# Down projections of a two-layer diffusion backbone as seven products instead of eight

## The chip, the cores and the metric

One core of one Trainium2 chip runs the whole program. The metric is the device time of one execution in microseconds (us). A profile of one execution gives the start and the length of every instruction on the engines: TensorE (PE; its weight loads are PEld), VectorE (DVE), ScalarE (ACT), GpSimd (POOL) and SyncE (SP).

## The reference, cut to what matters

The network has two layers over 512 latent tokens and 256 context tokens, 768 in all, with a width D of 1024. Each layer is a feed-forward half, a token mixer and a second feed-forward half. All three are modulated and normalised alike. The feed-forward part has 2816 features, in 22 tiles of 128:

```python
def _ffn_sublayer(h, shift, scale, gate, g_pre, g_post, w_gate, w_up, w_down):
    u = _modulate(_rmsnorm(h, g_pre), shift, scale)
    y = (jax.nn.silu(u @ w_gate) * (u @ w_up)) @ w_down
    return h + FFN_RES * gate * _rmsnorm(y, g_post)
```

The last layer's mixer and second feed-forward part need the 512 latent tokens alone. So of the four feed-forward parts three work on 768 tokens and the last on 512.

## The kernel before

Every float32 product runs as three passes: each operand is split into a leading part `hi`, made by a copy on ScalarE, and the rest `lo`, made by a subtraction on VectorE. TensorE then sums hi x hi, hi x lo and lo x hi in PSUM. Function `halves` (L191) does one split; `weights` (L177) loads a block of 128 rows and splits it 512 columns at a time.

A feed-forward part (`ffn`, L527) has two stages.

*Gate and up.* The first two feature tiles are ordinary products. The other twenty go through `strassen` (L588), two tiles at a time, by seven products in place of eight: the blocks are feature tile by half of D on one side and half of D by chunk of tokens on the other. A chunk is 384 tokens (256 in the last part). One `job` (L606) is one pair of tiles for gate or for up: two loads of weights, three splits, four sums of weights on VectorE, four more splits, seven products of 12 matmuls with 384 columns, and copies and sums of the results. 20 jobs make up a stage. Each feature tile's h goes to DRAM (`hd`).

*Down.* `type2` (L665) takes one chunk of tokens after the other. For each of the 22 feature tiles it loads 128 rows of `w_down` and the chunk's h from `hd`, splits both, and adds three passes into three accumulators of [128 tokens, 1024], 18 matmuls of 512 columns. The last four feature tiles (`STAG`) are held back and run token tile by token tile, so that the three token tiles of a chunk finish 24 matmuls apart. The last feed-forward part takes its four token tiles jointly.

*Boundary.* When a token tile is finished, `boundary` (L494) squares its two halves on ScalarE, multiplies them by the gate's row on VectorE, takes the root on GpSimd, and returns the rest: load x, add, store x, normalise (`normed`, L407: a square on ScalarE, a scaling on GpSimd), and `make_u` (L375): eight transposes on TensorE (`turned`, L416), shift and scale on ScalarE and VectorE, and the split into the next stage's u. The first chunk's rests are run between feature tiles of the second chunk (`later`); the second chunk's at once, beside the next stage's first products. Where the next stage is a feed-forward part, `Sums` (L422) also makes the differences of u that its seven products take; `prepare` adds hi and lo of the first chunk up again on GpSimd.

The order of instructions on each engine is chosen at compile time by a scheduler, from priorities and from when operands are ready. `late` (L81) makes an instruction keep its place behind those issued before it on its queue. Loads and the stores of h go through SyncE's queue; loads and stores of x and the gate's rows go through GpSimd's.

## Time and profile before

| | |
|---|---|
| device time, median of 3 runs | 2635.53 us (2626.84 to 2635.57) |
| span of the profiled execution | 2636.3 us |
| TensorE busy | 2546.2 us (97%) |
| VectorE busy | 1757.5 us (67%) |
| ScalarE busy | 1351.8 us (51%) |
| mean DMA rate | 153 GB/s |

The span runs from the first to the last instruction of the program, on the same clock as the device time. Busy time is the union of an engine's instructions; TensorE's overlap, and their ends are modelled.

### The profile page before, as it was taken

Reading aid. Unit: us, or ns where it says so; the run is one execution under the profiler, and the core shown is the slowest. Engines: PE = TensorE matmul, PEld = TensorE weight load, DVE = VectorE, ACT = ScalarE, POOL = GpSimd, SP = SyncE. Lnnn points to the kernel's source line nnn. Section 1 sums busy time; section 2 is a strip of 40 time slices with the busy share of each in tenths; the row PEclk is TensorE's granted clock in tenths of the full one; section 3 lists DMA queues with packets and bytes.
Section 4 is the critical chain, followed back from the end, with each engine's and each line's share of the span. In section 5 each row is a group of like instructions: output and inputs, shape, how many; then the busy total and the mean of one; then the engine's idle time right before and its main releaser. Section 6 shows DMA issues by size and latency. Waiting matters only on the chain.

```text
span 2636.3 us, 38740 instructions
## 1 busy us (share of the span) xinstructions
PE 2546.2 (97%) x13980; PEld 2237.5 (85%) x13980; DVE 1757.5 (67%) x3199; ACT 1351.8 (51%) x2783; POOL 325.3 (12%) x356
## 2 busy tenths in 40 slices
PE   7999999999999999999999999999999899899998
PEld 5899998889855789999888899998887667799986
DVE  5766664658777686767555767665557657899843
ACT  4444444547566654444454544444545556666632
POOL 4000000213022240000011300000122221400000
PEclk8999999999999999999999999999999999999999
DMA  7445436541387443232555332235554552544542
GB/s 275 144 160 168 152 127 206 192 160 53 119 293 266 157 141 96 96 105 100 187 184 189 124 97 95 98 107 177 198 181 152 200 176 82 177 135 128 161 167 88
DMA packets 147761, 403.00 MB, mean 153 GB/s; under 512 B 16504, under 2 KB 33576, under 8 KB 147568
## 3 DMA queue, kind: packets, MB, share of 16 engines
q1 hardware_dynamic: 136688, 362.00, 41.6%
q0 software_dynamic: 10880, 38.53, 4.2%
q8 instruction: 109, 1.79, 0.3%
q14 instruction: 84, 0.69, 0.1%
HBM read 351.91 MB, written 48.55 MB: 152 GB/s over the span
## 4 chain that ended last, share of the span: by engine, by line
PE 80%; DVE 7%; issue 5%; ACT 3%; POOL 3%; DMA 2%; POOLq 0%; DVEq 0%; ACTq 0%; SPq 0%
PE px L601 17%; PE py L601 12%; PE pz L601 12%; PE d110a L701 4%; PE d100a L701 4%; PE d000a L701 4%; PE d010a L701 4%; PE ada L122 3%; PE d001a L701 3%; PE d101a L701 3%; PE eo0a L701 1%; PE oq1a L701 1%; PE qkv1a L701 1%; PE opT L1286 1%; PE gu L201 1%
## 5 line engine op out<-in xcount | busy, mean ns | idle before, releaser
L210 POOL TENSOR_TENSOR b_0pr<-b_0pv,mhalf 128x1 f32<-128x1 f32 x4 | 2.2, 560 | 983.9 <-DVE b_0pv L208 983.9
L634 DVE TENSOR_TENSOR cp<-px,cp 128x384 f32<-128x384 f32 (+1 forms) x160 | 76.5, 520 | 56.3 <-PE px L601 56.3
L724 ACT ACTIVATE hh<-hr 128x384 fp32r<-128x384 f32 x132 | 68.6, 521 | 81.5 <-DMA hr<-hd 80.6
L725 DVE TENSOR_TENSOR hh<-hr,hh 128x384 fp32r<-128x384 f32 x132 | 72.9, 559 | 50.6 <-ACT hh L724 49.5
L636 ACT ACTIVATE h<-cp 128x384 f32<-128x384 f32 (+1 forms) x160 | 77.0, 498 | 26.1 <-DVE cp L634 21.9
L122 PE MATMUL ada<-wa,sc 128*32 128x512 f32 x512 | 83.8, 611 | 0.5 <-DVE cols L137 0.4
L634 DVE TENSOR_TENSOR cp<-pz,cp 128x384 f32<-128x384 f32 (+1 forms) x80 | 41.9, 524 | 57.4 <-PE pz L601 56.4
L638 DVE TENSOR_TENSOR h<-cp,h 128x384 f32<-128x384 f32 (+1 forms) x160 | 79.6, 519 | 0.4
L629 ACT ACTIVATE cp<-px 128x384 f32<-128x384 f32 (+1 forms) x160 | 71.4, 446 | 0.0
L634 DVE TENSOR_TENSOR cp<-py,cp 128x384 f32<-128x384 f32 (+1 forms) x80 | 41.7, 521 | 26.7 <-PE py L601 17.2
L614 DVE TENSOR_TENSOR w<-w,w 128x512 f32<-128x512 f32 x80 | 56.8, 709 | 1.6 <-DMA w<-in_wgu_dram 0.2
L193 DVE TENSOR_TENSOR d110w_0lo<-d110w,d110w_0hi 128x512 fp32r<-128x512 f32 x22 | 15.2, 691 | 63.6 <-ACT d110w_0hi L193 63.6
L617 DVE TENSOR_TENSOR w<-w,w 128x512 f32<-128x512 f32 x80 | 55.3, 691 | 2.0
L615 DVE TENSOR_TENSOR w<-w 128x512 f32<-128x512 f32 x80 | 55.2, 690 | 1.9
L616 DVE TENSOR_TENSOR w<-w,w 128x512 f32<-128x512 f32 x80 | 55.1, 689 | 1.5
L701 PE MATMUL d011a<-d011w_0hi,hh 128*128 128x512 f32 x132 | 52.7, 399 | 0.2 <-ACT hh L724 0.2
L701 PE MATMUL d101a<-d101w_0hi,hh 128*128 128x512 f32 x132 | 52.5, 398 | 0.0
L701 PE MATMUL d001a<-d001w_0hi,hh 128*128 128x512 f32 x132 | 52.5, 398 | 0.0
L701 PE MATMUL d100a<-d100w_512hi,hh 128*128 128x512 f32 x132 | 52.4, 397 | 0.0
L701 PE MATMUL d000a<-d000w_512hi,hh 128*128 128x512 f32 x132 | 52.4, 397 | 0.0
L701 PE MATMUL d010a<-d010w_0hi,hh 128*128 128x512 f32 x132 | 52.3, 396 | 0.0
L701 PE MATMUL d101a<-d101w_512hi,hh 128*128 128x512 f32 x132 | 52.2, 396 | 0.0
(5579 smaller groups left out, 9579.9 us busy)
## 6 DMA issues: line engine op xcount, KB each, us to landing
w<-in_wgu_dram SPq DMA_DIRECT2D x175, 512.0 KB, 3.5
wa<-in_w_ada_dram SPq DMA_DIRECT2D x204, 256.0 KB, 4.6
hd<-h SPq DMA_DIRECT2D x66, 384.0 KB, 4.7
hr<-hd SPq DMA_DIRECT2D x132, 192.0 KB, 3.7
wa<-in_w_ada_dram SPq DMA_DIRECT2D x42, 512.0 KB, 4.3
d000w<-in_w_down_dram SPq DMA_DIRECT2D x22, 512.0 KB, 3.5
d001w<-in_w_down_dram SPq DMA_DIRECT2D x22, 512.0 KB, 3.8
d010w<-in_w_down_dram SPq DMA_DIRECT2D x22, 512.0 KB, 3.9
```

The lines of the kernel that those rows point to most:

```text
L122: ins = nc.tensor.matmul(acc[32 * g:32 * g + 32, :], lhsT=self.sc[:, k, :], rhs=raws[g], start=(k == 0), stop=(k == KD - 1), skip_group_ch ...
L601: mm = lambda x, y, **kw: nc.tensor.matmul(out, lhsT=x, rhs=y, skip_group_check=True, **kw)
L614: nc.vector.tensor_sub(x3, x1, x3)
L615: nc.vector.tensor_add(x1, x1, x2)
L617: nc.vector.tensor_sub(x4, x4, x2)
L629: nc.scalar.activation(t, src, AF.Copy)
L634: nc.vector.tensor_add(t, acc, t)
L636: nc.scalar.activation(hc, t, AF.Silu)
L638: nc.vector.tensor_mul(hc, t, hc)
L701: mm(acc[:, h:min(h + 512, n)], lhsT=x[xi][:, js], rhs=w[h // 512][wi], start=(k == 0 and xi == 0 and wi == 0), stop=(k == nk - 1 and xi = ...
L724: self.nc.scalar.activation(t[:, 0], src, AF.Copy)
L725: self.nc.vector.tensor_sub(t[:, 1], src, t[:, 0].bitcast(F32))
```

## The change

*Down.* In the three feed-forward parts of 768 tokens the down product is also cut into blocks: chunk of tokens by feature tile of a pair on one side, feature tile of the pair by half of D on the other. `down` runs seven products over the 11 pairs, one after the other, each for three token tiles into three banks of PSUM. Four of the weight blocks are sums, which `down_sums` makes on VectorE during gate and up from rows loaded through GpSimd's queue (`down_load`); they go to DRAM (`wt`). The sums of h are made by `h_sums` when a pair of tiles is ready; they go to `hd`, which now has four blocks a pair. The first chunk's tiles are finished after the fifth product, the second chunk's after the seventh; each half of a tile goes through `half` (square, gate) when it is there. In the first and last feature tiles of a product the matmuls run token tile by token tile. Operands are loaded and split two feature tiles at a time, at least `AHEAD` = 4 feature tiles early.

*Order.* `chain` makes each instruction follow the last one given to the same chain on its engine. ScalarE's and VectorE's instructions of gate and up stand in one chain each, written out so that a job makes the next job's operands between its own copies and sums; so do the splits, copies and sums of down, and its loads on SyncE.

*Merged splits.* `weights` and the jobs split 1024 columns in one instruction where they split 512 twice. Results of two token chunks are added, activated or multiplied together (768 columns). The loads of later modulation weights are 512 KB instead of two of 256 KB.

*Boundary.* `boundary` now returns two parts: up to the normalisation, and the transposes with what follows. In down the six parts of the first chunk stand at fixed places of the sixth product, and their transposes keep their place in TensorE's order.

*u in float32.* The first chunk's u stays in float32 where `Sums` needs it; `prepare` is gone. The second chunk's tiles of u are allocated when its first token tile is finished, since `down` keeps sums in their place. The area for descriptors of GpSimd's transfers is given as 8192 bytes.

The core of the diff, mostly its new functions:

```diff
+    def chain(self, last, ins):
+        e = ins.ins.engine
+        if e in last:
+            self.tc.add_manual_dep(ins.ins, last[e], mybir.DependencyInfo(
+                mybir.DependencyClass.NoSync, mybir.DependencyReason.DATA), reason="chain")
+        last[e] = ins.ins.name
...
     def weights(self, src, name):
-        raw = self.raw(src, name)
+        hi, lo = self.split(self.raw(src, name), name)
         n = src.shape[-1]
-        return [self.split(raw[:, i:min(i + 512, n)], f"{name}_{i}") for i in range(0, n, 512)]
...
+    def wtiles(self, n, name, one=False):
+        return [self.ws.tile([P, n], F32R, tag=("o" if one else "w") + e, bufs=2 if one else 4, name=name + e) for e in ("hi", "lo")]
...
+    def boundary(self, t, g, xsrc, xdst, nxt, name):
...
+        def half(i, y):
+            nc.scalar.activation(self.junk(f"{name}{i}")[:, cut[i]], y, AF.Square, accum_out=ss[:, i:i + 1])
+            nc.vector.tensor_mul(y1[:, cut[i]], y, g[:, cut[i]])
+        def end():
+            nc.vector.tensor_add(ss[:, 0:1], ss[:, 0:1], ss[:, 1:2])
+            r = self.rms_r(ss[:, 0:1], D, name + "p")
+            def rest():
+                x = bp.tile([P, D], F32, tag="bx", bufs=2, name=name + "x")
+                nc.gpsimd.dma_start(x, xsrc(t))
+                for c in cut if nxt is None else [slice(0, D)]:
+                    nc.vector.scalar_tensor_tensor(x[:, c], y1[:, c], r[:, 0:1], x[:, c], op0=ALU.mult, op1=ALU.add)
+                    if nxt is None:
+                        nc.sync.dma_start(xdst(t)[:, c], x[:, c])
+                if nxt is not None:
+                    nc.gpsimd.dma_start(xdst(t), x)
+                    self.normed(x, y1, name + "u")
+            return rest, lambda: nxt and self.make_u(y1, t, *nxt, name + "u")
+        return half, end
...
+    def down_sums(self, b, wt, chain):
+        nc = self.nc
+        (b11, b12), (b21, b22) = ((x[:, 0:512], x[:, 512:]) for x in b)
+        chain(nc.vector.tensor_add(b11, b11, b12))
+        chain(nc.vector.tensor_add(b12, b12, b22))
+        self.late(nc.gpsimd.dma_start(wt[0], b[0]))
+        chain(nc.vector.tensor_add(b22, b11, b22))
+        chain(nc.vector.tensor_add(b21, b22, b21))
+        self.late(nc.gpsimd.dma_start(wt[1], b[1]))
+    def h_sums(self, h, n, hd, nm, joint, chain=lambda ins: ins):
+        nc = self.nc
+        a11, a21, a12, a22 = (x[:, c * n:(c + 1) * n] for x in h for c in range(2))
+        nc.sync.dma_start(hd[1], h[1])
+        if joint:
+            nc.sync.dma_start(hd[0], h[0])
+            return
+        s12 = self.bp.tile([P, 2, n], F32, tag="by", bufs=3, name=f"hs{nm}")
+        s4 = self.junk(f"hs{nm}")[:, 0:n]
+        chain(nc.vector.tensor_sub(s12[:, 0], a22, a21))
+        chain(nc.vector.tensor_sub(a21, a11, a21))
+        nc.sync.dma_start(hd[0], h[0])
+        minus = lambda out, x, y: chain(nc.vector.scalar_tensor_tensor(out, x, -1.0, y, op0=ALU.mult, op1=ALU.subtract))
+        minus(s12[:, 1], s12[:, 0], a11)
+        nc.sync.dma_start(hd[2], s12.rearrange("p c n -> p (c n)"))
...
+        wd = self.a["w_down"][l, s].rearrange("(q e r) d -> e r q d", e=2, r=P)
+        raw = lambda e, h: lambda q: wd[e][:, q, h * 512:(h + 1) * 512]
+        mod = lambda e, h: lambda q: wt[q, e][:, :, h * 512:(h + 1) * 512].rearrange("q r d -> r q d")
+        blk = lambda i, c: lambda q: hd[q, i][:, :, c * n:(c + 1) * n].rearrange("q r n -> r q n")
+        self.psum_phase()
+        bank = lambda t: [self.pp.tile([P, 512], F32, tag=t, bufs=m, name=f"{t}{l}{s}{j}") for j in range(m)]
+        k12 = self.up.tile([P, 2, m, 512], F32, tag="u1h", name=f"k12{l}{s}")
+        u5 = self.up.tile([P, m, 512], F32, tag="u1l", name=f"k5{l}{s}")
+        jobs, todo, ready, chained = [], [], {}, {}
+        chain = lambda ins: self.chain(chained, ins)
+        def halves(hi, lo, x):
+            chain(nc.scalar.activation(hi, x, AF.Copy))
+            chain(nc.vector.tensor_sub(lo, x, hi.bitcast(F32)))
+        def product(a, b, acc, first, done):
+            jobs.append((acc, first, done))
+            todo.extend((len(jobs) - 1, q, a, b) for q in range(0, np_, 2))
+        def make():
+            i, p, a, b = todo.pop(0)
+            nm = f"{l}{s}{i}_{p}"
+            if hook and (i, p) == (5, 4):
+                hook()
+            w = min(2, np_ - p)
+            q = slice(p, p + w)
+            ar = self.c3([P, w, n], F32, f"dh{nm}")
+            chain(nc.sync.dma_start(ar, a(q)))
+            tag, bufs = ("bx", 2) if i < 5 and p // 2 % 3 == 2 else ("raw", 3)
+            br = self.ws.tile([P, w, 512], F32, tag=tag, bufs=bufs, name=f"dw{nm}")
+            chain(nc.sync.dma_start(br, b(q)))
+            ah, al = (self.c3([P, w, n], F32R, f"dh{nm}{e}") for e in "hl")
+            halves(ah, al, ar)
+            bh, bl = (t.rearrange("p (e n) -> p e n", e=w) for t in self.wtiles(w * 512, f"dw{nm}s"))
+            halves(bh, bl, br)
+            for e in range(w):
+                ready[i, p + e] = p + e, (ah[:, e], al[:, e]), (bh[:, e], bl[:, e])
+        def run():
+            steps = [(i, p) for i in range(len(jobs)) for p in range(np_)]
+            parts = {(5, q): e for q, e in ((0, (0, 0)), (2, (1, 0)), (4, (0, 1)), (5, (2, 0)), (7, (1, 1)), (9, (2, 1)))}
+            held = []
+            for k, (i, p) in enumerate(steps):
+                a = min(k + self.AHEAD, len(steps) - 1, (i + 1) * np_ + 1 if p > np_ - 4 else len(steps))
+                while todo and steps[a] not in ready:
+                    make()
+                if (i, p) in parts:
+                    j, f = parts[i, p]
+                    ends[0, j][f]()
+                acc, first, done = jobs[i]
+                acc = acc() if callable(acc) else acc
+                jobs[i] = acc, first, done
+                held.append(ready[i, p])
+                end = np_ - (5 if i == len(jobs) - 1 else 3)
+                if p == 0 or end <= p < np_ - 1:
+                    continue
+                for j in range(m):
+                    for e in held:
+                        mms(acc[j], e, j, first)
+                    if p == np_ - 1:
+                        done(j, acc[j])
+                held = []
+        def mms(out, e, j, first):
+            p, x, w = e
+            js = slice(j * P, (j + 1) * P)
+            for xi, wi in ((0, 0), (0, 1), (1, 0)):
+                nc.tensor.matmul(out, lhsT=x[xi][:, js], rhs=w[wi], start=first and p == 0 and xi == wi,
+                                 stop=p == np_ - 1 and xi == 1, skip_group_check=True)
+        def keep(to):
+            return lambda j, acc: chain(nc.scalar.activation(to[:, j], acc, AF.Copy))
+        def minus(x, acc):
+            chain(nc.vector.scalar_tensor_tensor(x, acc, -1.0, x, op0=ALU.mult, op1=ALU.subtract))
+        ends = {}
+        def left(j, acc):
+            chain(nc.vector.tensor_add(k12[:, 0, j], acc, k12[:, 0, j]))
+            ends[0, j] = start(0, j, g)
+            ends[0, j][0](0, k12[:, 0, j])
+        def right(j, acc):
+            minus(k12[:, 1, j], acc)
+            ends[0, j][0](1, k12[:, 1, j])
+            ends[0, j] = finish(0, j, ends[0, j][1], True)
+        def right2(j, acc):
+            minus(u5[:, j], acc)
+            ends[1, j] = start(1, j, g)
+            ends[1, j][0](1, u5[:, j])
+        def left2(j, acc):
+            ends[1, j][0](0, acc)
+            finish(1, j, ends[1, j][1])
+        x, z = bank("dx"), []
+        product(blk(0, 0), raw(0, 0), x, True, keep(k12[:, 0]))
+        product(blk(1, 0), raw(1, 0), lambda: bank("dy"), True, left)
+        product(blk(2, 1), mod(1, 1), x, False, keep(k12[:, 1]))
+        product(blk(2, 0), mod(0, 0), lambda: z.extend(bank("dy")) or z, True, keep(u5))
+        product(blk(3, 0), raw(1, 1), lambda: z, False, right)
+        product(blk(0, 1), mod(0, 1), x, False, right2)
+        product(blk(1, 1), mod(1, 0), x, False, left2)
...
+        def made(p, b):
             nm = f"{l}{s}{p}{b}"
+            w = {}
             r1, r2 = (self.raw(self.a["wgu"][l, s, 2 * p + e, b], f"w{nm}{e}") for e in range(2))
+            w["a11"], w["a12"] = cut(split(r1, nm + "a1"))
+            w["a22"] = split(r2[:, 512:], nm + "a22", True)
+            yield w
             x3, x4, x1, x2 = r1[:, 0:512], r1[:, 512:], r2[:, 0:512], r2[:, 512:]
+            chain(nc.vector.tensor_sub(x3, x1, x3))
...
                 if b == 0:
+                    chain(nc.scalar.activation(hc, cp[f], AF.Silu))
                 else:
+                    chain(nc.vector.tensor_mul(hc, cp[f], hc))
+            (u1, u2), (u4, u5) = ([t[:, c] for c in range(2)] for t in cp)
+            product(x, w["a11"], b11, True)
+            copy(u1, x)
+            after = step()
+            product(y, w["a12"], b21, True)
+            chain(nc.vector.tensor_add(u1, y, u1))
+            step()
+            product(z, w["s1"], t1, True)
+            copy(u5, z)
+            product(x, w["s2"], t2, False)
+            copy(u2, x)
+            step()
+            product(z, w["s4"], b22, False)
+            chain(nc.vector.tensor_add(u2, z, u2))
+            out(0)
...
+        wb = None if joint else self.down_load(l, s, 0)
+        def between(p, b):
+            nonlocal wb
+            if joint or (b and p != NF // 2 - 2):
+                return
+            r = p - 1 + b if p < NF // 2 - 1 else p
+            self.down_sums(wb, wt[r], chain)
+            if r < NF // 2 - 1:
+                wb = self.down_load(l, s, r + 1)
+        for i, (p, b) in enumerate(jobs):
+            if b == 0:
+                h = [self.c3([P, 2 * n], F32, f"h{l}{s}_{2 * p + e}") for e in range(2)]
+            nxt = made(*jobs[i + 1]) if i + 1 < len(jobs) else iter(())
+            w = job(p, b, h, w, nxt, lambda: between(p, b))
+            if b:
+                self.h_sums(h, n, hd[p], f"{l}{s}{p}", joint, chain)
+        if joint:
+            self.psum_phase(True)
```

## Rows read from the trace of the kernel before

**Rows 1.** The page's busy times: us, share of the span, instructions.
```profile
PE 2546.2 (97%) x13980; PEld 2237.5 (85%) x13980; DVE 1757.5 (67%) x3199; ACT 1351.8 (51%) x2783; POOL 325.3 (12%) x356
```

**Rows 2.** Busy time by stretch: length; each engine; granted clock, DMA share, GB/s.
```profile
core 0: us, PE busy (x) PEld busy (x) DVE busy (x) ACT busy (x) POOL busy (x), PEclk, DMA share, GB/s
392.70:577.10 184.40, 184.01 (x801) 148.13 (x799) 99.22 (x200) 85.63 (x170) 16.92 (x25) 1.00 0.57 190
...
981.50:1272.70 291.20, 291.20 (x1682) 291.20 (x1681) 201.91 (x338) 141.90 (x266) 0.00 (x0) 1.00 0.32 102
...
1507.20:1804.00 296.80, 296.80 (x1682) 296.80 (x1681) 201.91 (x338) 141.83 (x266) 0.00 (x0) 1.00 0.31 101
```

**Rows 3.** Groups of TensorE in the first chunk's down products: busy, mean ns, idle.
```profile
L701 PE MATMUL d000a<-d000w_512hi,hh 128*128 128x512 f32 x132 | 52.4, 397 | 0.0
...
L701 PE MATMUL d000a<-d000w_0lo,hh 128*128 128x512 f32 x66 | 26.1, 396 | 0.0
```

**Rows 4.** Timeline of TensorE in a down stage: start us, us, instruction.
```profile
516.22 0.40 PE L701 MATMUL d001a<-d001w_0hi,hh 128*128 128x512 f32 x1
516.45 0.40 PE L701 MATMUL d001a<-d001w_512hi,hh 128*128 128x512 f32 x1
```

**Rows 5.** The chain that ended last: start us, us, what.
```profile
392.84 92.41 PE d000a L701 x396
...
994.18 4.16 PE px L601 x24
...
1520.05 4.24 PE px L601 x24
```

**Rows 6.** Groups of VectorE and ScalarE: busy, mean ns, idle before and releasers.
```profile
L725 DVE TENSOR_TENSOR hh<-hr,hh 128x384 fp32r<-128x384 f32 x132 | 72.9, 559 | 50.6 <-ACT hh L724 49.5
...
L634 DVE TENSOR_TENSOR cp<-px,cp 128x384 f32<-128x384 f32 x120 | 61.4, 553 | 53.0 <-PE px L601 53.0
L614 DVE TENSOR_TENSOR w<-w,w 128x512 f32<-128x512 f32 x80 | 56.8, 709 | 1.6 <-DMA w<-in_wgu_dram 0.2
...
L193 DVE TENSOR_TENSOR d000w_0lo<-d000w,d000w_0hi 128x512 fp32r<-128x512 f32 x22 | 15.2, 692 | 30.2 <-ACT d000w_0hi L193 30.2
...
L724 ACT ACTIVATE hh<-hr 128x384 fp32r<-128x384 f32 x132 | 68.6, 521 | 81.5 <-DMA hr<-hd 80.6 <-POOL tab L1132 0.4 <-DVE d101w_512lo L193 0.4
```

**Rows 7.** DMA issues: count, KB each, median us to landing.
```profile
w<-in_wgu_dram SPq DMA_DIRECT2D x175, 512.0 KB, 3.5
...
hr<-hd SPq DMA_DIRECT2D x132, 192.0 KB, 3.7
...
d000w<-in_w_down_dram SPq DMA_DIRECT2D x22, 512.0 KB, 3.5
```

**Rows 8.** Timelines of VectorE, ScalarE and TensorE behind the second down stage.
```profile
1475.16 1.27 DVE L514 SCALAR_TENSOR_TENSOR b_5x<-b_5y,b_5pr,b_5x 128x1024 f32<-128x1024 f32 x1
...
1465.79 1.06 ACT L410 ACTIVATE b_4y<-b_4x 128x1024 f32<-128x1024 f32 x1 [1.23 <-DVE b_4x L514]
...
1469.22 0.58 ACT L505 ACTIVATE b_5q<-d011a 128x512 f32<-128x512 f32 x1
...
1458.48 1.09 PE L419 MATMUL b_3utp<-ident,b_3y 128*128 128x128 f32 x8 [0.94 <-POOL b_3y L414]
...
1470.61 1.09 PE L419 MATMUL b_4utp<-ident,b_4y 128*128 128x128 f32 x8 [1.86 <-POOL b_4y L414]
1481.67 1.97 PE L419 MATMUL b_5utp<-ident,b_5y 128*128 128x128 f32 x8 [3.25 <-POOL b_5y L414]
```

**Rows 9.** Waits of TensorE: us in total, times, longest.
```profile
PE b_5utp L419 <- POOL b_5y L414: 8.0, 4, 3.2
PE b_4utp L419 <- POOL b_4y L414: 7.9, 5, 2.4
...
PE b_3utp L419 <- POOL b_3y L414: 3.8, 4, 0.9
...
PE oq1a L701 <- DVE oq1w_512lo L193: 1.7, 1, 1.7
```

More of the change, by code (lines that the diff above doesn't have):

```diff
@@ L30 @@
     STAG = 4
+    AHEAD = 4
     def __init__(self, tc, a, out, stop=99):
@@ new lines, in job @@
+            step()
+            product(z, w["s4"], b22, False)
+            chain(nc.vector.tensor_add(u2, z, u2))
+            out(0)
+            step()
+            product(y2, w["a22"], t4, True)
+            copy(u4, y2)
+            between()
+            product(x, w["s3"], t3, False)
+            chain(nc.vector.tensor_add(cp[1], x.unsqueeze(1).to_broadcast([P, 2, n]), cp[1]))
+            out(1)
+            return after
+        self.psum_phase()
+        jobs = [(p, b) for p in range(1, NF // 2) for b in range(2)]
```

211 lines of the change are left out of this document (103 added, 108 removed).

## The prediction

> **What bounds the kernel now.** I read the busy shares first, then the stages one by one, then the spacing of the matmuls inside a stage, and last what TensorE waits for. TensorE is busy for 97% of a span of 2636.3 us [rows 1]. An average can hide a stage with another limit, so the stages come next: in the gate-and-up stages (the 291.2 us from 981.5 us on, for example) and in the down stages (184.4 us from 392.7 us on) TensorE has work in all but a few tenths of a microsecond, while VectorE is busy for 201.9 of 291.2 us and 99.2 of 184.4 us, ScalarE for about half or less, and the transfers take 101 to 190 GB/s [rows 2]. So in both stages it is the number of TensorE instructions that sets the time, not the supply.
>
> A matmul's duration must not be used as its price. A 512-column down matmul is drawn 0.40 us long, but the next one starts 0.23 us later, because they overlap [rows 3, 4]. The price is the spacing: 396 of them in 92.41 us, 0.2333 us each [rows 5]. For 384 columns it is 4.16/24 = 0.173 us; in the third gate-and-up stage, with the same instructions, it is 4.24/24 = 0.177 us [rows 5], so that stage takes 296.8 us where the one before took 291.2 us [rows 2]. I know no cause for that and come back to it in the range.
>
> **The term that carries the sum.** A down projection of 768 tokens is 22 feature tiles x 6 token tiles x 2 halves of D x 3 passes = 792 matmuls; one chunk has 396 of them, in groups like the two shown [rows 3, 5]. Three of the four feed-forward layers take the new form; the last one, whose down products come as one joint pass, keeps the old. Seven products of 11 feature pairs x 3 token tiles x 3 passes are 693. So 99 matmuls go in each of three layers, 297 in all, each 512 columns wide as before. At the spacing: 297 x 0.2333 = **69.3 us** less. The cover of this term is nothing: TensorE has no idle time there to absorb it.
>
> [...] This case's row has 233 ns over 396 matmuls at full granted clock [rows 2, 5], and it decides for 69.3 us.
>
> **What the seven products add elsewhere.** (a) In gate and up VectorE gets four sums of 512 columns for each pair of weight tiles, 0.71 us each [rows 6], 11 pairs: 31 us; and four of 384 columns for each pair of feature tiles, 0.56 us each [rows 6], 11 pairs: 25 us. 201.9 + 56 = 258 of 291 us: still under TensorE. The price is zero while the fixed order lets VectorE use its gaps. (b) The traffic there: 22 loads and 22 stores of 512 KB on GpSimd's queue and 1.5 blocks more of h per pair, about 30 MB in 291 us, on top of 101 GB/s [rows 2]: some 200 GB/s, about what the down stages already move. Zero; were a load late, VectorE would wait for it at its sum, with the last product's addition queued behind, which is the VectorE rival below. (c) In down, two feature tiles now take 18 matmuls, 4.2 us, as before, with 512 KB of weights and 384 KB of h: 218 GB/s against 190 [rows 2]. Loads landed in 3.5 to 3.7 us [rows 7], and three to four pairs of buffers run ahead. Zero, with a doubt that is a rival below.
>
> **The seven borders of a layer.** At a product's end its results are copied or added in a fixed order with the operand splits, and the second pair of the next product is split only behind them. Counted from the last matmul: ScalarE's copy of 512 columns 0.6 us, its splits of 768 and 1024 columns 0.9 and 1.06 us, and VectorE's last split 1.27 us [rows 6, 8] (the 768 lies between the 384 of 0.52 and the 1024 of 1.06) is 3.8 us, and some tenths of hand-over. TensorE meanwhile has the first pair, 18 matmuls, 4.2 us. So the cover just holds where nothing else is in VectorE's order; where a gate multiplication of 0.69 us falls in between, it is missed by about half a microsecond. From below: 0. From above: two such multiplications, 1.4 us at 21 borders, 29 us. I take 0.3 us on average, nearer the end that the sum of rows gives: **+6 us**.
>
> **Boundaries.** The first chunk's tiles are now turned three to four pairs of products (6 to 8 us) after their normalisation was begun, in a fixed place of TensorE's order, and the gate's loads lie far ahead. The second chunk's three tiles finish 15 matmuls apart (3.5 us) instead of 24 (5.6 us), so the first of them starts its chain 4 us nearer the end; against that, half of each tile has been squared and scaled one product earlier, which takes a ScalarE and a VectorE step of 0.6 and 0.7 us out of each. The old chain is slow: the last tile's second half was squared at 1469.22 us, its sum with x came at 1475.16 us and its transposes at 1481.67 us [rows 8], with 16.6 us of next-stage products over it. TensorE's waits for tiles 3, 4 and 5 were 19.7 us in the whole run [rows 9], 6.05 us of them behind the second down stage [rows 8]; for the three down stages together I take twice that, 12 us. Bounds: all 12 gone, or 3 us more at each; I take +1 us each and +1 us for waits of the first chunk's turns: **+4 us**.
>
> **Edits with one answer.** A split of 1024 columns instead of two of 512: two back-to-back 512s on VectorE are 2 x 0.69 us [rows 6] against 1.27 us [rows 8], nothing for a busy engine; but the first use comes some 0.45 us later. That counts only where TensorE waits for a split, as it does in the mixers' projections (1.7 us at one place [rows 9]): bounds 0 and 4 us, I take **+1.5 us**. Keeping the first chunk's u in float32 drops GpSimd additions that work beside the down products, where TensorE is not idle: 0. The wider copies, adds and gate multiplications of gate and up, and the order on ScalarE and VectorE, work on engines with slack: 0. The wider loads of the modulation weights carry the same bytes: 0. The smaller buffer for descriptors: 0; GpSimd's transfers are spread over 291 us.
>
> Sum against the profiled execution: 2636.3 - 69.3 + 6 + 4 + 1.5 = 2578.5 us. The median of the runs shown is 2635.5 us, 0.8 us under that span: **2578 us**.
>
> **Rivals.**
> *Little stalls at the borders and tidier boundaries.* The border costs are 0, and the new order takes half to all of the 12 us of boundary waits: 2636 - 69 - 6 to -12 gives 2554 to 2561 us. For it: the splits can run ahead wherever the copies are early. Against: VectorE's work per boundary tile hardly shrinks. 18%.
> *Borders cost 1 to 2 us each.* 21 x 1.5 = 32 us: about 2604 us. For it: one VectorE multiplication too many uses up the cover. 14%.
> *VectorE sets gate and up.* 258 of 291 us leave 33 us a layer; in a fixed order its waits (behind the product px alone it idled for 53.0 us [rows 6]) may no longer be filled. If a job ran 0.5 us long, 60 jobs cost 30 us: about 2608 us; it takes 1.1 us a job to eat the whole gain (about 2640 us). 8%, of which 3 reach no change.
> *Slower: the loads stand behind the border.* If the next product's second pair were loaded only when the border's order lets it, then 3.7 us of landing [rows 7] and the 3.8 us of the border chain come against 4.2 us of cover, plus SyncE's place in line: 3.3 us a border is the point at which 69.3 us are gone; 4.5 us would give 2636 - 69 + 95 = 2662 us. Against it: buffers come free at the split, so loads can be three pairs ahead. 4%.
> *A saved matmul is worth less.* The saving is 69 us only if each matmul that goes takes its whole spacing with it. [...] The 396 equal spacings of the row [rows 5] exclude it but for 1%. [...]
>
> **How the numbers follow.** The forecast as summed has 55%, with its own range 2564 to 2592 us. The spacing is the other unknown: the 1.9% between two equal stages [rows 5] may vanish (-6 us) or come to another stage (+6 us each, +3 us for a down stage). The range that leaves out no more than 2 in 10 takes in the first rival and most of the second: 2552 to 2610 us. A measurement of this kernel can tell about 0.5% (13 us) from no change. Faster: 55 + 18 + 14 + 5 + 1 = 93%; the 3% of the VectorE rival give no change; 4% slower.
>
> **What would show it.** Right: 693 matmuls in each of three down stages, some 162 us long and 2 to 4 us of transposes, spacing still 0.233 us; gate and up still near 291 us with VectorE near 255 us; waits of TensorE under half a microsecond at product borders. Wrong: the spacing has changed; TensorE waits at the borders for a split of the second pair or for a landing; jobs of gate and up are longer than 14.6 us; or the next stage's first tiles wait longer for tiles 3 to 5.

## The result, and the profile after

The changed kernel takes 2671.51 us (median of 4 runs, 2669.37 to 2673.87), the kernel before 2631.74 us beside it on the same chip: a ratio of 1.0147, 95% interval 1.0122 to 1.0173. It is slower by some 40 us where 2578 us was forecast. The profiled execution spans 2667.6 us against 2636.3 us.

The busy times of the page of the changed kernel:

```profile
PE 2514.8 (94%) x13683; PEld 2202.9 (83%) x13683; DVE 1877.3 (70%) x2840; ACT 1279.6 (48%) x2240; POOL 371.1 (14%) x472
```

The 297 matmuls are gone [rows 1], but TensorE's share has fallen from 97% to 94%: it waits where it did not before. Where, the stretches tell. These are the changed kernel's first down stage, second gate-and-up stage, third down stage and last gate-and-up stage (columns as in [rows 2]):

```profile
core 0: us, PE busy (x) PEld busy (x) DVE busy (x) ACT busy (x) POOL busy (x), PEclk, DMA share, GB/s
390.90:566.10 175.20, 167.67 (x718) 132.81 (x717) 111.74 (x173) 92.61 (x141) 16.79 (x24) 0.99 0.67 234
985.80:1281.80 296.00, 296.00 (x1681) 296.00 (x1681) 238.10 (x320) 123.89 (x184) 23.53 (x44) 1.00 0.55 199
...
1801.00:1984.00 183.00, 168.38 (x718) 133.80 (x717) 111.72 (x145) 90.32 (x139) 26.93 (x35) 0.96 0.65 221
2309.25:2534.15 224.90, 207.85 (x1682) 200.76 (x1680) 176.60 (x239) 108.98 (x184) 0.00 (x0) 1.00 0.37 121
```

And the kernel before in its last gate-and-up stage, a stretch that the prediction did not look at:

```profile
2299.60:2500.90 201.30, 198.84 (x1683) 198.02 (x1681) 183.59 (x343) 129.83 (x269) 0.00 (x0) 1.00 0.44 138
```

Gate and up with 384 columns went as forecast: TensorE without a gap, VectorE 238 of 296 us, 199 GB/s. The down stages are shorter (to its last matmul the first of them takes 190.1 us in the kernel before; the 184.4 us of [rows 2] stop some 5.7 us short of it), but hold 7.5 us and 14.6 us without TensorE work. And the last gate-and-up stage, with 256 columns a chunk, has become some 25 us longer, up to the first matmul of the next stage, although VectorE and ScalarE both have less to do in it.

Laid end to end, from the first instruction of a stretch to the first of the next on TensorE, in us (E2, E6 and E12 are experiments below; a down stage goes with what follows it up to a fixed mark: the mixer's first products, the next stage's seven products, and for the third the odd mixer's output projection, so that the odd mixer is in it):

| stretch | before | changed | E2 | E6 | E12 |
|---|---|---|---|---|---|
| three gate-and-up stages of 384 columns | 902.4 | 904.3 | 904.3 | 904.2 | 903.9 |
| three down stages and what follows each | 874.1 | 858.8 | 836.3 | 841.7 | 813.0 |
| even mixer up to its output projection | 244.6 | 247.7 | 244.6 | 244.6 | 244.1 |
| both output projections up to gate and up | 200.2 | 219.9 | 221.4 | 200.1 | 203.1 |
| last gate-and-up stage | 201.3 | 226.5 | 209.2 | 203.1 | 202.7 |
| opening, last down stage, tail | 213.7 | 210.5 | 209.7 | 209.5 | 209.9 |
| span | 2636.3 | 2667.6 | 2625.4 | 2603.1 | 2576.7 |

So the down stages with what follows them gained 15 us in place of the 59 of the forecast (69.3 less 6 and 4), and 20, 25 and 3 us were lost in stretches that the forecast had at 1.5 us together.

**The last gate-and-up stage.** What TensorE waits for there, in the changed kernel (us in total, times, longest):

```profile
PE px L781 <- ACT cp L828: 8.7, 9, 1.6
PE pz L781 <- ACT cp L828: 5.5, 9, 1.0
PE py L781 <- ACT cp L828: 2.1, 8, 0.3
```

A timeline of one such wait, TensorE and ScalarE:

```profile
2401.84 0.28 PE L781 MATMUL pz<-t0h,1150s12lo 128*128 128x256 f32 x1
...
2405.14 0.63 ACT L792 ACTIVATE 1151a22hi<-w 128x512 fp32r<-128x512 f32 x1 [3.35 <-DMA w<-in_wgu_dram]
2405.68 0.37 ACT L828 ACTIVATE cp<-pz 128x256 f32<-128x256 f32 x1
2405.94 0.38 ACT L828 ACTIVATE cp<-px 128x256 f32<-128x256 f32 x1
...
2406.10 0.39 PE L781 MATMUL pz<-u_1h,1150s34hi 128*128 128x256 f32 x1 [1.04 <-ACT cp L828]
```

The product in pz is finished at 2402.1 us. Its copy is a matter of 0.37 us, and ScalarE has nothing to do; but the written order puts the split of the next job's weights in front of it, and that split stands 3.35 us for a load. TensorE must add to pz next and waits 1.04 us. The listed waits are 16.3 us; matmuls are drawn longer (0.28 us here) than their spacing (0.118 us), so part of each pause is hidden. Counted from start to start, 75 steps of over 0.2 us hold 26 us more than that spacing each (2.6 us in the kernel before).

**The third down stage.** The seams look like this, GpSimd, TensorE and ScalarE of the changed kernel:

```profile
1922.56 1.52 POOL L218 TENSOR_TENSOR b_2pr<-b_2pv,mhalf 128x1 f32<-128x1 f32 x1 [1.54 <-DVE b_2pv L216]
1924.03 2.17 POOL L1350 DMA_DIRECT2D gains<-in_qkgain_dram  x4
...
1929.70 1.40 POOL L1357 TENSOR_TENSOR tab<-rope,gains 128x256 f32<-128x256 f32 x2 [1.32 <-DMA rope<-in_rope_glb_dram]
...
1931.68 1.13 POOL L428 TENSOR_SCALAR b_0y<-b_0x,b_0ur 128x1024 f32<-128x1024 f32 x1
...
1932.86 0.48 PE L433 MATMUL b_0utp<-ident,b_0y 128*128 128x128 f32 x1 [5.50 <-POOL b_0y L428]
...
1942.38 0.80 PE L727 MATMUL dx<-dw_4shi,dh_4h 128*128 128x512 f32 x1 [7.55 <-ACT dw_4shi L667]
```

The odd mixer's gains and rope tables (the hook of the sixth product) come in front of the scaling of the first tile on GpSimd; the tile's transposes have a fixed place on TensorE, which stands 5.50 us; then the splits of the next pair have queued behind the rest of the boundary, and it stands another 7.55 us. The granted clock of this stage is 0.96: after the 5.50 us in which TensorE stood, it is 0.50 from 1934 to 1944 us.

### The profile page after: what moved, and what is told of

The parts are those of the page before. It is cut to its first block, busy times and chain, and to the rows that moved or that the text cites. A ratio compares the mean times of both kernels' runs of the same rounds, so it can differ in the third digit from the quotient of the medians.

```text
span 2667.6 us, 36586 instructions
## 1 busy us (share of the span) xinstructions
PE 2514.8 (94%) x13683; PEld 2202.9 (83%) x13683; DVE 1877.3 (70%) x2840; ACT 1279.6 (48%) x2240; POOL 371.1 (14%) x472
## 4 chain that ended last, share of the span: by engine, by line
PE 72%; DVE 10%; issue 6%; DMA 5%; ACT 4%; POOL 2%; SPq 0%; POOLq 0%; DVEq 0%; ACTq 0%
PE px L781 14%; PE py L781 9%; PE pz L781 9%; PE dy L727 8%; PE dx L727 7%; PE d11a L926 4%; PE ada L129 3%; DMA w<-in_wgu_dram 2%; PE oq1a L926 1%; PE gu L209 1%; PE gu L210 1%; PE gu L208 1%; PE eo0a L926 1%; PE qkv1a L926 1%; DMA dw<-in_w_down_dram 1%
## 5 line engine op out<-in xcount | busy, mean ns | idle before, releaser
L828 ACT ACTIVATE cp<-px 128x384 f32<-128x384 f32 (+1 forms) x160 | 73.3, 458 | 209.7 <-PE px L781 209.2
L834 ACT ACTIVATE h<-cp 128x768 f32<-128x768 f32 (+1 forms) x80 | 63.4, 793 | 222.5 <-DVE cp L858 153.5
L858 DVE TENSOR_TENSOR cp<-px,cp 128x768 f32<-128x768 f32 (+1 forms) x80 | 70.7, 884 | 4.0 <-PE px L781 4.0
L836 DVE TENSOR_TENSOR h<-cp,h 128x768 f32<-128x768 f32 (+1 forms) x80 | 71.3, 891 | 2.5
L828 ACT ACTIVATE cp<-pz 128x384 f32<-128x384 f32 (+1 forms) x80 | 36.7, 459 | 72.5 <-PE pz L781 72.1
L611 POOL DMA_DIRECT2D wt<-in_w_down_dram x66 | 35.4, 537 | 112.5 <-DMA wt<-wt 112.5
L1315 POOL TENSOR_SCALAR p<-p,sm 128x256 f32<-128x256 f32 (+2 forms) x48 | 32.4, 688 | 133.3 <-DVE sm L1312 66.8
L828 ACT ACTIVATE cp<-py 128x384 f32<-128x384 f32 (+1 forms) x80 | 36.0, 450 | 13.9 <-PE py L781 13.6
L1214 ACT ACTIVATE optb<-opT 128x512 fp32r<-128x512 f32 x48 | 28.6, 596 | 28.2 <-PE opT L1511 27.8
L1301 DVE TENSOR_REDUCE mx<-s 128x1 f32<-128x512 f32 (+2 forms) x40 | 27.4, 686 | 19.0 <-PE s L1292 13.3
L1215 DVE TENSOR_TENSOR optb<-opT,optb 128x512 fp32r<-128x512 f32 x48 | 33.1, 689 | 11.0 <-ACT optb L1214 10.6
```

What stands on the lines that cost most here:

```text
L828: chain(nc.scalar.activation(t, src, AF.Copy))
L834: chain(nc.scalar.activation(hc, cp[f], AF.Silu))
L836: chain(nc.vector.tensor_mul(hc, cp[f], hc))
L858: chain(nc.vector.tensor_add(cp[1], x.unsqueeze(1).to_broadcast([P, 2, n]), cp[1]))
```

## The experiments

All are edits of the changed kernel. The ratios are to the kernel before, which took 2627.6 us beside E1 to E4, 2634.0 us beside E5 to E8 and 2630.9 us beside E9 to E12 (medians), with single runs from 2623 to 2643 us. Small differences between runs of different groups therefore rest on the stretches of their traces.

| run | what is edited | median, us | ratio, 95% interval |
|---|---|---|---|
| E1 | last gate and up without written order | 2646.49 | 1.006 [1.0034, 1.0087] |
| E2 | splits and buffers of 512 again | 2625.85 | 0.9985 [0.9969, 1.0001] |
| E3 | down by eight products again | 2709.26 | 1.0301 [1.0264, 1.0339] |
| E4 | first chunk's transposes not pinned | 2676.64 | 1.0183 [1.0153, 1.0214] |
| E5 | first chunk's u not kept in float32 | 2658.0 | 1.0096 [1.0073, 1.0119] |
| E6 | E1, E2 and E5 together | 2606.47 | 0.9901 [0.9879, 0.9922] |
| E7 | E6, no written order in any gate and up | 2672.65 | 1.0159 [1.0131, 1.0188] |
| E8 | E6, boundary spread, tables moved | 2586.48 | 0.9825 [0.9803, 0.9847] |
| E9 | splits of 512 into buffers of 1024 | 2636.31 | 1.0019 [1.0001, 1.0037] |
| E10 | E6, tables moved | 2598.22 | 0.9873 [0.9834, 0.9913] |
| E11 | E6, down by eight products again | 2634.19 | 1.0011 [0.9992, 1.003] |
| E12 | E8, u in float32 at the down boundary | 2579.25 | 0.9804 [0.9757, 0.9851] |

**E1, the order of the last gate and up.**

```diff
-        chain = lambda ins: self.chain(last, ins)
+        chain = (lambda ins: ins) if joint else lambda ins: self.chain(last, ins)
```

> The changed kernel, but in the last feed-forward layer's gate and up (256 columns a chunk, jobs of about 10 us) ScalarE's and VectorE's instructions are no longer tied into the written order. Theory (the fixed order puts the copies of finished products behind splits of weights, and TensorE's next product into the same bank waits for the copy; in this stage a job is 10 us long, so the waits are not covered): first job to first joint down matmul falls from about 225 to about 201 us, the waits of TensorE on the copies go, and the run is some 24 us faster than the changed kernel: about 2645 us. Rival (the wider results and merged buffers, not the order, make the waits): within 5 us of the changed kernel, about 2670 us.

25 us faster than the changed kernel; the stretch falls from 226.5 to 199.3 us, and of the 16.3 us of waits on copies 0.6 us are left. The theory holds. The order is not the only way out of these waits, though: E2 brings back 17 us of the same stretch with the order left in, and both together 23 us (E6), so the gains of E1 and E2 can't be added. (TensorE's own products may change places too in this run.)

**E2, the merged splits.** Each split of 1024 columns becomes two of 512, each into a buffer of its own (eight of 512 in place of four of 1024); the loads of the later modulation weights are 256 KB again too:

```diff
-        return [self.ws.tile([P, n], F32R, tag=("o" if one else "w") + e, bufs=2 if one else 4, name=name + e) for e in ("hi", "lo")]
...
+        return [[self.ws.tile([P, 512], F32R, tag="w" + e, bufs=8, name=f"{name}{i}{e}") for i in range(n // 512)] for e in ("hi", "lo")]
```

> The changed kernel with weights split 512 columns at a time again, into eight buffers of 512 in place of four of 1024, in gate and up, the down projections, the mixers' projections and the modulation weights. Theory (the two output projections lost 10 and 9 us because a split of 1024 columns delays the first use and holds back the next split until a whole buffer is free): the output projections come back by 10 to 20 us together; but gate and up and down have more instructions in their written order, each about 0.1 us dearer for the halves, so the total is 2650 to 2665 us. Rival (the output projections lost their time to the first chunk's turned tiles at a fixed place of TensorE's order): they stay at about 127 and 93 us, and the run is 2670 us or slower.

46 us faster, much more than expected, and not where I had looked: the output projections stay at 221 us (128.0 and 93.3), as the rival had it. The rival's reason is not borne out: with the transposes free (E4) they take 125.9 and 93.5 us. The gain is in the last gate and up (17 us), in the down stages and what follows them (22 us) and in the even mixer (3 us).

**E9, length of the instruction or size of the buffer.** The buffers stay at 1024 columns; only the instruction is halved:

```diff
-            chain(nc.scalar.activation(hi, src, AF.Copy))
-            chain(nc.vector.tensor_sub(lo, src, hi.bitcast(F32)))
+            for i in range(0, src.shape[-1], 512):
+                cols = slice(i, i + 512)
+                chain(nc.scalar.activation(hi[:, cols], src[:, cols], AF.Copy))
+                chain(nc.vector.tensor_sub(lo[:, cols], src[:, cols], hi[:, cols].bitcast(F32)))
```

> The changed kernel with its four buffers of 1024 columns kept, but each split made as two instructions of 512 columns. It separates the two sides of the merged splits. If the length of the instruction is the cost (a copy that TensorE waits for stands behind a split of 1.06 us, and the first use comes after the whole split): near the run with weights split by 512 throughout, 2626 to 2635 us, and the last gate and up near 209 us. If the size of the buffer is the cost (a buffer comes free only when both its halves have been used): near the changed kernel, 2660 to 2671 us, and the last gate and up near 226 us.

35 of the 46 us come back with the shorter instruction alone (ratios 1.0019 against 0.9985): the last gate and up takes 209.2 us as in E2, the down stages 171.9, 170.5 and 180.0 us as in E2 (172.6, 170.3, 180.0). The other 10 us lie in the mixers (the even mixer takes 253.5 against 244.6 us in E2, the way from the third down stage to the odd output projection 232.5 against 226.8, and the output projections give 6 us back). There the size of the buffers is left as a cause, or the loads of the modulation weights, which E2 halves and E9 does not; no run separates the two.

How the length reaches TensorE shows in the changed kernel's last gate and up:

```profile
2412.20 1.04 ACT L792 ACTIVATE 1151s34hi<-w 128x1024 fp32r<-128x1024 f32 x1
...
2413.28 1.22 DVE L793 TENSOR_TENSOR 1151s34lo<-w,1151s34hi 128x1024 fp32r<-128x1024 f32 x1 [1.65 <-ACT 1151s34hi L792]
2414.42 0.68 DVE L858 TENSOR_TENSOR cp<-px,cp 128x512 f32<-128x512 f32 x1
...
2415.14 0.63 ACT L834 ACTIVATE h<-cp 128x512 f32<-128x512 f32 x1 [1.62 <-DVE cp L858]
2415.68 0.37 ACT L828 ACTIVATE cp<-px 128x256 f32<-128x256 f32 x1
...
2416.09 0.39 PE L781 MATMUL px<-t1h,1151s12hi 128*128 128x256 f32 x1 [0.83 <-ACT cp L828]
```

VectorE's addition of the finished product px stands behind a whole split of the next job's weights, first ScalarE's part and then its own; ScalarE's activation waits for that addition, the copy of the next result in px stands behind the activation, and TensorE waits for the copy. This comes back in every second job. With splits of 512 the listed waits on px fall from 8.7 to 2.3 us and those on py from 2.1 us to nothing (E9). For the down stages and what follows them the runs show the gain, but no such chain was followed there.

**E3, the seven products taken out.**

```diff
-        self.down(l, s, n, hd, wt, self.load_gate(*gate), start, finish, hook)
+        for c in range(2):
...
+            self.type2(f"d{l}{s}{c}", NF, lhs, len(tiles[0]), lambda k: self.a["w_down"][l, s, k * P:(k + 1) * P, :], fin,
+                       hook=hook if c == 1 else None)
```

> The changed kernel with the three down projections by eight products again (type2, as before), without the sums of weights and of h and without their transfers; everything else of the change stays. Theory (seven products save 39 of 69 us in the down stages, the other 30 us are stalls of TensorE inside the products): down stages of 184 to 190 us, run about 2671 + 39 = 2710 us; if the sums of weights and of h cost gate and up something as well, a little less, about 2700 us. Rival (the seven products bring nothing, or lose, once what they move into gate and up and into the boundary is counted): 2671 us or faster.

38 us slower, so within the change the seven products are a gain, and the kernel with everything else of the change takes some 82 us more than the kernel before (2709 against 2628 us). The size is not as expected: the first and third down stages take 189.6 us each, but the second 209.1, where TensorE stands for splits of h (us in total, times, longest):

```profile
PE d011a L940 <- ACT hh L963: 9.8, 3, 3.4
```

In the kernel before and in E11 the second stage takes 190.6 and 190.5 us. So about half of the 38 us is this stall and not the worth of the products. By the code, this stage is the only one of the three behind which u is kept in float32, in the slots from which these splits are drawn too.

**E4, the pinned transposes.**

```diff
-            tp = self.turned(self.ps(name + f"tp{h}"), z, h, c == 0)
+            tp = self.turned(self.ps(name + f"tp{h}"), z, h)
```

> The changed kernel, but the transposes of the first chunk's tiles are no longer kept at their written place in TensorE's order. Theory (TensorE stood 2.9 and 5.5 us before the first tile's transposes in two down stages and 8.5 us before a tile's in the odd output projection, because they stand at a fixed place and the tile's scaling on GpSimd comes late): 8 to 17 us faster than the changed kernel, 2654 to 2663 us. Rival (behind the transposes the splits of the same boundary on ScalarE and VectorE are late too, so that TensorE waits for those instead): within 5 us of the changed kernel.

5 us slower; the third down stage grew to 190.8 us, and TensorE still stands 5.7 us before the first tile's transposes and 9.6 us before the third's. Neither side is right: the fixed place is not the cost by itself, and the waits have not moved to the splits (the wait of 7.6 us for them fell to 2.4). What is late is the scaling on GpSimd in front of the transposes.

**E5, u in float32.** GpSimd adds hi and lo of the first chunk again once its tiles are done:

```diff
-        if sums is not None and c == 0:
-            ut = sums.first[j] = [self.c3([P, 4, P], F32, f"{name}b{h}") for h in range(2)]
...
+                if sn is not None and (c, j) == (0, len(tl[s][0]) - 1):
+                    self.later.append(sn.prepare)
```

> The changed kernel, but the first chunk's u is no longer kept in float32 from the boundary on: GpSimd adds hi and lo once the chunk's tiles are done, as before the change. Theory (the kept tiles take 4 or 6 of the 23 shared slots earlier, so that the splits of the second half's attention outputs can no longer run ahead of the output projections, and TensorE waits for them): the even and the odd output projection with what leads to gate and up fall from 127 and 93 us to about 117 and 84 us, and the run is 15 to 20 us faster than the changed kernel, about 2653 us. Rival (the output projections lose their time to the merged boundary code or the order of the turns): they stay at 127 and 93 us and the run stays within 5 us of 2671 us.

13 us faster; the output projections fall from 126.8 and 93.0 to 119.9 and 89.8 us, half of what was expected. With E2's edit, which alone does nothing for them, they come back whole (E6: 116.1 and 84.0). ScalarE in the even output projection of the changed kernel, with the wait on TensorE:

```profile
902.42 1.48 ACT L409 ACTIVATE b_0ub<-b_0utp,cols,gs 128x128 f32<-128x128 f32 x4
903.79 0.53 ACT L949 ACTIVATE oh<-ya 128x384 fp32r<-128x384 f32 x1
...
904.37 0.82 PE L926 MATMUL eo1a<-eo1w1hi,oh 128*128 128x512 f32 x2 [1.91 <-ACT oh L949]
...
914.61 1.06 ACT L201 ACTIVATE eo1w6hi<-eo1w 128x1024 fp32r<-128x1024 f32 x1 [3.14 <-PE eo1a L926]
915.57 1.49 ACT L409 ACTIVATE b_1ub<-b_1utp,cols,gs 128x128 f32<-128x128 f32 x4
916.94 0.53 ACT L949 ACTIVATE oh<-ya 128x384 fp32r<-128x384 f32 x1
```

The splits oh of the mixer's outputs come one by one behind the tiles b_0ub, b_1ub that are now kept. In E6 the first oh of this stretch comes at 909.63 us, after all three tiles of the chunk: those before it had been split ahead.

```profile
905.58 1.49 ACT L415 ACTIVATE b_2uut<-b_2utp,cols,gs 128x128 f32<-128x128 f32 x4
...
909.63 0.51 ACT L972 ACTIVATE oh<-ott 128x384 fp32r<-128x384 f32 x1
```

That it is the 23 shared slots (both kinds of tile are drawn from them) which force this order is read from the code; no run here separates it from other reasons for the order. The stall of E3 fits it.

**E6, the three together.**

> The changed kernel with three undone together: weights split 512 columns at a time, no written order in the last layer's gate and up, the first chunk's u not kept in float32. If the three add up: 2626 (weights) - 8 (what is left of the last layer's 209 against 201 us) - 18 (output projections) = about 2600 us, faster than both kernels. If the slots are not what holds the output projections: about 2618 us.

2606 us, 19 us below E2 and faster than both kernels: the sum expected is missed by 6 us. Against E2 the output projections give 21 us and the last gate and up 6, and the down stages with what follows them take 5 us more.

**E7, the written order in the stages of 384 columns.** An edit of E6.

```diff
-        chain = (lambda ins: ins) if joint else lambda ins: self.chain(last, ins)
+        chain = lambda ins: ins
```

> The same three undone, and the written order of ScalarE and VectorE taken away in all four gate-and-up stages, not only in the last. Theory (in the stages of 384 columns VectorE has cover for its order): within 5 us of the kernel with the three undone, gate-and-up stages still 296 us. Rival (the order is what brings 259 us of VectorE work into a 296 us stage): jobs grow, 10 us or more slower.

My theory fell: 66 us slower than E6. The three stages take 338.7, 308.1 and 311.1 us in place of 312.5, 295.8 and 295.8, 54 us together; another 9 us lie ahead of the first of them. With the sums of weights and of h in them they need the order; the last stage, which has none of these sums and jobs of 10 us, is harmed by it.

**E8 and E10, the seams of the seven products.** Both are edits of E6. E10 moves only the tables; E8 moves the first chunk's turns too, and with the last of them GpSimd's additions of u, by two pairs:

```diff
-            if hook and (i, p) == (5, 4):
+            if hook and (i, p) == (6, 4):
...
-            parts = {(5, q): e for q, e in ((0, (0, 0)), (2, (1, 0)), (4, (0, 1)), (5, (2, 0)), (7, (1, 1)), (9, (2, 1)))}
+            parts = {(5, q): e for q, e in ((0, (0, 0)), (2, (1, 0)), (5, (0, 1)), (6, (2, 0)), (8, (1, 1)))}
+            parts[6, 1] = 2, 1
```

> The kernel with three edits undone (2606 us), with only the odd mixer's gains and rope tables moved from the sixth to the seventh product, the turns at the places of the change. If the loads and products of these tables in front of the boundary scaling on GpSimd made the stalls of the third down stage: that stage falls from 180 to about 170 us, first and second stay at 173 and 175 us, run about 2596 us. If the places of the turns did: the third stage stays near 180 us, run about 2606 us.

> The same three undone, and in the down projections the first chunk's boundary spread further: its turns one to three pairs later (the third tile's in the seventh product) and the odd mixer's gains and rope tables loaded in the seventh product in place of the sixth. Theory (the stalls of 4.4 and 7.5 us in the third down stage are the boundary scaling on GpSimd queued behind these loads and products, with the turns at fixed places): third down stage falls from 180 to about 170 us, first and second to 168 to 170 us, 10 to 15 us faster than the kernel with the three undone. Rival (a fixed cost at the seams of the products): down stages unchanged within 2 us each.

With the tables alone the third down stage falls from 179.9 to 169.3 us, and the first, which has a hook of its own at that place, from 172.6 to 169.5 us; 4 us are given back on the way to the odd output projection (231.3 against 227.1), and the run is 8 us faster (the two runs' intervals in the table overlap; the stretches show it). With the turns spread as well the stages take 167.6, 171.8 and 167.7 us, and it is 20 us faster than E6. Both causes are real; the rival of a fixed cost at the seams is out.

**E12, what E8 left in the second down stage.** An edit of E8. VectorE, GpSimd and TensorE of E8 there:

```profile
1397.79 0.96 DVE L682 TENSOR_TENSOR dh_0l<-dh,dh_0h 128x768 fp32r<-128x768 f32 x1
...
1404.34 5.84 DVE L682 TENSOR_TENSOR dh_2l<-dh,dh_2h 128x768 fp32r<-128x768 f32 x1
...
1404.36 5.00 POOL L458 TENSOR_TENSOR b<-u_0h,u_0l 128x512 f32<-128x512 f32 x4
...
1411.44 0.79 PE L745 MATMUL dx<-dw_2s0lo,dh_2h 128*128 128x512 f32 x1 [4.13 <-DVE dw_2s0lo L682]
```

The same split takes 0.96 us and 5.84 us. E12 takes the additions away from this place (u stays in float32 at the down boundary, as in the change) and keeps them behind the mixers:

```diff
-        ut = bp.tile([P, KD, P], F32, tag="bu", bufs=2, name=name + "ut")
+        if sums is not None and c == 0 and sums.keep:
+            ut = sums.first[j] = [self.c3([P, 4, P], F32, f"{name}b{h}") for h in range(2)]
...
+                if sn:
+                    sn.keep = s == 2
```

> The kernel with the spread boundary (2586 us), with the first chunk's u kept in float32 at the down boundary but made by GpSimd additions behind the mixers. In the spread kernel a VectorE split of 768 columns took 5.84 us instead of 0.96 us in the second down stage, exactly while GpSimd ran four of these additions (5.00 us). Theory (the additions hold VectorE up): the wait of 4.1 us goes, the second down stage falls from 172 to about 167 us, run about 2582 us. Rival (chance neighbours, or the slots taken earlier cost the same): within 2 us of 2586 us.

The second down stage falls from 171.8 to 165.5 us and the run to 2579 us. It is the fastest kernel here, 2% under the one before (1.5 to 2.4%). Its three down stages:

```profile
390.44:557.25 166.81, 165.31 (x718) 132.07 (x717) 113.10 (x206) 94.48 (x176) 18.33 (x24) 1.00 0.71 242
1256.09:1421.60 165.51, 165.19 (x718) 132.30 (x717) 109.28 (x177) 93.20 (x174) 15.09 (x18) 1.00 0.70 241
1761.89:1929.54 167.65, 165.50 (x718) 132.28 (x717) 111.00 (x176) 93.05 (x173) 27.48 (x34) 1.00 0.71 241
```

TensorE is busy for all but 0.3 to 2.2 us. And the chain of E12 that ended last shows the price of a matmul (start, us, what):

```profile
390.60 23.09 PE dx L747 x99
413.70 23.10 PE dy L747 x99
```

**E11, the worth of the seven products without the rest.** E6 with E3's edit.

> The kernel with three edits undone, and the down projections by eight products again. It measures what the seven products are worth where the other edits cost little. The kernel with three undone has down stages of 173, 175 and 180 us against 190 us: theory, 43 us in the down stages and a few given back at the boundaries, so this run takes 2606 + 38 to 45, about 2648 us, slower than the kernel before (2634 us) by the spacing of the second gate-and-up stage (5 us) and the boundary code. Rival (the sums and their transfers slow gate and up or the boundary): less than 30 us above 2606 us.

2634 us, no different from the kernel before, so what is left of the other edits is neutral in sum. Against E6 the seven products are worth 28 us, which is the rival's side: 43 us in the stages (570.8 against 527.5), 17 given back behind them. Of the rival, the boundary holds; gate and up is not slowed (904.2 us in E6, 905.6 in E11). Against E12 they are worth 55 us: 70.8 us in the stages, 15.6 given back behind them; that takes in E12's u at the down boundary, which E11 does not have.

## Why the prediction was wrong

**Right: the term that carried the sum.** 297 matmuls went, and the spacing stayed: 23.10 us for 99 is 0.2333 us. E12's down stages are 70.8 us shorter than E11's where 69.3 us was forecast; together with what follows them they gain 61.2 us over the kernel before (874.1 to 813.0), where 59.3 us was forecast. The rival by which a saved matmul is worth less is out. So are late loads at the borders: in E12 the rows of h and of `w_down` take 6.8 us to land (median), not the 3.5 to 3.7 us of the forecast, and the stages move 241 GB/s, but TensorE has hardly a gap. That the change came out slower had 4%, and by this rival's mechanism; the way it did come about was in none of the rivals.

**Right: the sums and their traffic in gate and up.** VectorE 238 us where I had 258, 199 GB/s where I had 200, no gap of TensorE. But E7 shows that the price of zero holds only with the fixed order: without it these stages cost 54 us and the run 66.

**Wrong, first: "Edits with one answer", the merged splits.** I priced a split of 1024 columns by its own time, "nothing for a busy engine", and by a first use 0.45 us later, at 1.5 us of a possible 4. Measured: 46 us (E2), of which 35 are the length of the instruction (E9). The 0.45 us counted the leading part alone: the rest `lo` comes only after both instructions, 1.05 and 1.22 us for 1024 columns against 0.62 and 0.68 for 512, about 1 us later. And what counts more than the split is what stands behind it in the order of its engine: in the timeline under E9 VectorE starts its addition at 2414.42 us, when the split of 1.22 us from 2413.28 us on is all but over. For the last gate and up the rows of E9 show these to be the additions and copies that free a bank; for the boundaries it is argued from the place of the gain. VectorE's busy time in the last gate and up did fall (183.6 to 176.6 us), and the stage grew.

**Wrong, second: "the order on ScalarE and VectorE, work on engines with slack: 0".** I looked for slack in the stages of 384 columns [rows 2], 202 of 291 us, and not in the last one, where VectorE was busy for 183.6 of 201.3 us and a job lasts 10 us. The order costs 25 us there with splits of 1024 columns (E1), and 6 us with splits of 512 (E2 against E6). My rival "VectorE sets gate and up" had the mechanism, a fixed order whose waits can't be filled, but in the stages where the order in fact helps.

**Wrong, third: u in float32 at 0.** I counted the GpSimd additions that go, not the tiles that stay: 13 us alone (E5), and 21 us of the output projections from E2 to E6. Nor was the cover what I said. In the second down stage the additions do cost, 6.3 us (E12): beside them a VectorE split takes 5.84 us (E8), without them 0.95 us (E12). There the edit is right.

**Mis-sized: the borders (+6) and the boundaries (+4).** As the change places them, turns and tables cost 20 us (E6 to E8). Placed well, the borders cost nothing of the 6 (E12's stages are 1.5 us better than the term alone); what follows the stages takes 9.7 us more than in the kernel before (313.0 to 303.3 us) in place of 4.

The steps from the changed kernel to E12 add up: 46 (E2), 19 (E6), 8 (E10), 12 (E8), 7 (E12) are 92 us, 2671 to 2579 us; the last 7 undo there what E6 had brought back with E5's edit. That 2579 us is within 1 us of the sum forecast for the change as a whole is partly luck: the borders came 7.5 us better than their term and what follows the stages 5.7 us worse.

**Open.** A matmul of 384 columns took 4.16/24 us in the second gate-and-up stage of the kernel before and 4.24/24 in its third [rows 5]; in the changed kernel, E11 and E12 all stages have 4.24/24. It costs the second stage 4.8 us (291.2 to 296.0). Since E11 has it too, it isn't the seven products; no run here tells what it is. Nor can one trace of the kernel before tell whether its scatter (2623 to 2643 us, where no edited kernel spreads over more than 8.3) is this spacing.

## What to carry to other kernels

Price a merged or reordered instruction by what is queued behind it on its engine, and look up that price in the tightest stage that the same code serves, not in the longest. An engine with slack on average is no cover where a bank or a buffer is needed within a few microseconds: in the last gate and up ScalarE was busy for 109.0 of 224.9 us, and TensorE waited 16.3 us for its copies. And when a change with a sound main term loses, undo its side edits one by one before giving it up: here the main term was worth 55 us, and undoing or moving what came with it brought 92.

## What the runs showed of the hardware

At three places instructions of GpSimd and VectorE took longer beside each other, at two of them through more than one instruction of the other. In E8 one VectorE split of 768 columns took 5.84 us instead of 0.96 us beside four GpSimd additions of 5.00 us in all, and ended 0.8 us after the last of them; in E12, which has no additions at this place, the same split took 0.95 us. In the kernel before one addition is enough: at 915.32 us a split of 512 columns took 1.79 us instead of 0.69 us beside an addition of 1.49 us, and ended 0.5 us after it. It goes the other way too: in the changed kernel GpSimd's scaling of 1024 columns at 1942.92 us took 2.43 us instead of the 1.12 us of the one at 1933.43 us, while VectorE ended one split and ran a whole second one, and it ended 0.9 us after that. The rows do not show how the two hold each other up, nor who issued first: by its recorded start VectorE's split came 0.02 us before the first addition in E8 and 0.24 us after the addition in the kernel before, and it took longer both times.
